# Two products per block of keys in the attention of the second block: both parts of a head's values in one loaded weight

## The chip, the cores and the metric

The kernel runs on one core of one Trainium2 chip. The metric is the device time of one execution in microseconds (us): three executions gave 2305.38, 2310.02 and 2313.08, so the median is 2310.02.

## What is computed

The reference is two transformer blocks one after the other, on 512 tokens of width 1024, in float32. The first block (a gated convolution and a linear recurrence, then a layer of 16384 experts) is not touched. The second block has two attentions side by side, which the code calls A and B, then two gated branches, an output projection and a SwiGLU layer.

```python
def forgetting_attention(q, k, v, log_f):        # A: 8 heads of 64
    c = jnp.cumsum(log_f, axis=1)
    s = einsum('bqhd,bkhd->bhqk', q_i, k) * scale + (c_q - c_k), causal mask
    p = jax.nn.softmax(s, axis=-1)
    return einsum('bhqk,bkhd->bqhd', p, v)

def latent_attention(q_nope, q_rope, k_nope, k_rope, v):   # B: 8 heads, values of 64
    s = (einsum('bqhd,bkhd->bhqk', q_nope, k_nope) + einsum('bqhr,bkr->bhqk', q_rope, k_rope)) * scale
    p = jax.nn.softmax(where(chunk mask, s, NEG_INF), axis=-1)
    return einsum('bhqk,bkhd->bqhd', p, v)
```

## The kernel before

TensorE multiplies in a float32 format that keeps fewer bits than float32. So each operand is split (`split`, lines 93 to 95) into an upper part, which ScalarE rounds and copies, and a lower part, which VectorE forms as the difference. A product of two operands is made of three (`mm3`, lines 111 to 121): upper weight by upper data on line 117, upper weight by lower data on line 119, lower weight by upper data on line 120, all summed in PSUM. Each of them loads its own 128 columns of weights.

`second` (from line 1065) runs the second block. Attention A: for each half of four heads it projects q, k and the values (`va_proj`, split on line 1259), then calls `attend` for each head. The values of a half lie in one tile of 4 x 512 columns (`va`, lines 1236 to 1238): first the upper parts of all four heads, 256 columns for each of the four blocks of 128 keys, then the lower parts. A head is read as the 128 columns of its pair of heads (`d`, line 1287), so that the product gives both heads of the pair on 128 rows, and 64 of these are kept. Attention B: the values of all eight heads are projected in four steps and split whole (512 columns, line 1310) into one tile of upper and one of lower parts (`vb`), and again the pair is read. Each head of B first makes its own q (two blocks of the projection, then the rotation `rope`) and k.

`attend` (lines 1031 to 1063) does one head. For each of four blocks of 128 queries: the logits `S` (three products), the biased logits into a tile `lg` (in A the bias is written into `lg` first, line 1282), the largest, the exponential on ScalarE, the reciprocal on VectorE, the scaling on GpSimd (line 1051), transposes of 128 x 128 into `pt` (line 1054), and the split of `pt` into the tiles `ph` and `pl`. The tile `lg` comes out of a ring of five, `S` and `pt` have two banks of PSUM each, `ph`, `pl` and `o` have one. Then the products with the values go into `o`: for each of the four blocks of keys three products over the 512, 384, 256 and 128 queries that can see that block, 12 products in all. At last ScalarE copies the 64 rows of the head out of `o` (line 1063).

Between the heads stands other work of TensorE: the projections of the gates (`gate_tiles`, two of 24 products for each listed head, `GATE_A` and `GATE_B`), which are started behind the first product of `S` and of `o` of their head (`self.anchor`, an order alone, no wait), the projections of the second half of A, and those of B. The order of the instructions on each engine is planned at build time by the framework's own model of the time line, from the order of the program and from when it thinks operands are ready; the order that is built is then fixed.

Of the kernel before, what the change touches and what calls it, by code (L numbers as in the profile page):

```python
# [7 lines left out]
F32 = mybir.dt.float32  # L8
F32R = mybir.dt.float32r
# [3 lines left out]
AF = mybir.ActivationFunctionType  # L13
ALU = mybir.AluOpType
# [4 lines left out]
P = 128  # L19
T = 512  # L20
# [50 lines left out]
class K:  # L71
# [11 lines left out]
    def v(self, name, i=0, n=1):  # L83
        o, w = VOFF[name]
        return self.vec[:, o + i:o + i + n]
# [944 lines left out]

    def attend(self, q, k, v, nq, scale, bias, out, row, pools):

        nc = self.nc
        wk, pss, pst, psv, unit = pools
        ph, pl = unit("ph").bitcast(F32R), unit("pl").bitcast(F32R)
        for qt in range(nq):
            n = (qt + 1) * P
            s = slice(qt * P, n)
            S = pss.tile([P, T], F32, name="S")
            first = self.mm3(S[:, :n], [(q[0][:, s], q[1][:, s], k[0][:, :n], k[1][:, :n])])  # L1040
            if qt == 0:
                self.anchor = [first]
            lg = wk.tile([P, T], F32, name="lg", bufs=5)
            sm = wk.tile([P, 4], F32, name="sm", bufs=5)
            nc.vector.tensor_tensor_reduce(lg[:, :n], S[:, :n], bias(qt, lg), scale=1.0, scalar=NEG, op0=ALU.add,
                                           op1=ALU.max, accum_out=sm[:, 0:1])
            nc.vector.tensor_scalar(sm[:, 1:2], sm[:, 0:1], -scale, None, op0=ALU.mult)
            nc.scalar.activation(lg[:, :n], lg[:, :n], AF.Exp, bias=sm[:, 1:2], scale=scale,
                                 accum_out=sm[:, 2:3])
            nc.vector.reciprocal(sm[:, 3:4], sm[:, 2:3])  # L1050
            nc.gpsimd.tensor_tensor(lg[:, :n], lg[:, :n], sm[:, 3:4].to_broadcast([P, n]), op=ALU.mult)
            pt = pst.tile([P, 4, P], F32, name="pt", tag="pt")
            for kb in range(qt + 1):
                nc.tensor.transpose(pt[:, kb], lg[:, kb * P:(kb + 1) * P], self.ident)
            self.split(ph[:, :qt + 1, s], pl[:, :qt + 1, s], pt[:, :qt + 1])
        o = psv.tile([P, T], F32, name="o", tag="o")
        for kb in range(nq):
            vh, vl = v(kb)
            s = slice(kb * P, T)
            first = self.mm3(o[:, s], [(vh, vl, ph[:, kb, s], pl[:, kb, s])], start=kb == 0, stop=kb == nq - 1)  # L1060
            if kb == 0:
                self.anchor.append(first)
        nc.scalar.activation(out, o[row:row + 64], AF.Copy)

    def second(self):
        nc, tc, a = self.nc, self.tc, self.a
        hh, hl, x2 = self.hh, self.hl, self.x2
        NQ = T // P
# [4 lines left out]
        with ExitStack() as octx:  # L1073
            op = self.pool("s0", 1, ctx=octx)
            wk = self.pool("swk", 2, ctx=octx)
# [8 lines left out]
            def unit(tag):  # L1084
                return up.tile([P, 4, T], F32, name="u" + tag, tag=tag)
# [33 lines left out]
            for z in range(2):  # L1119
                for tt in range(NQ):  # L1120
                    nc.tensor.matmul(st[:, z, tt:tt + 1], acc[z][:, tt * P:(tt + 1) * P], self.ones[:, :1],
                                     start=True, stop=True)
# [108 lines left out]
            qa, ka, va = [], [], []  # L1231
            for pr in range(4):
                t = unit(f"{pr}").bitcast(F32R)
                qa.append((t[:, 0], t[:, 1]))
                ka.append((t[:, 2], t[:, 3]))
            for half in range(2):
                t = unit(f"v{half}").bitcast(F32R).rearrange("p a (b d) -> p (a b) d", d=256)
                va.append((t[:, :NQ], t[:, NQ:]))

            def qk(dst, scale):  # L1240
                def fn(n, ps):
# [5 lines left out]
            def va_proj(blk):  # L1247
                raw = self.wload(a["w_in2"][6 + blk], 2048)
                w = []
                for z in range(2):  # L1250
                    h, l = self.wsplit(raw[:, z * 1024:(z + 1) * 1024])
                    w += [(h[:, i * 256:(i + 1) * 256], l[:, i * 256:(i + 1) * 256]) for i in range(4)]
                for tt in range(NQ):
                    s = slice(tt * P, (tt + 1) * P)
                    ps = bank(1 + 2 * (tt % 2))
                    self.mm3(ps[:, :256], [(hh[:, k, s], hl[:, k, s], w[k][0], w[k][1]) for k in range(KT)])
                    t = wk.tile([P, 256], F32, name="vt", tag="t3", bufs=3)
                    nc.vector.tensor_scalar(t, ps[:, :256], rt[:, 2, tt:tt + 1], None, op0=ALU.mult)
                    self.split(va[blk][0][:, tt], va[blk][1][:, tt], t)

            for half in range(2):
                if half == 0:
                    for n in range(2):
                        qk(ka, 1.0)(n, zs[4 + n])
                else:
                    self.proj([a["w_in2"][4]], KT, hh, hl, qk(ka[2:], 1.0), lambda n: bank(1 + 2 * n))
                self.proj([a["w_in2"][3 + 2 * half]], KT, hh, hl, qk(qa[2 * half:], 0.125), lambda n: bank(1 + 2 * n))
                va_proj(half)
                for h in range(4 * half, 4 * half + 4):
                    pr, row = h // 2, 64 * (h % 2)  # L1270
                    pq = pr - 2 * half

                    if h == 0:
                        nb = psx.tile([P, T], F32, name="nb", tag="x")
                        nc.tensor.matmul(nb, self.ident[:8, h:h + 1].to_broadcast([8, P]), n8, start=True, stop=True)
                    else:
                        nb = wk.tile([P, T], F32, name="nb")
                        nc.sync.dma_start(nb, n8d[h:h + 1].to_broadcast([P, T]))

                    def bias(qt, b):  # L1280
                        n = (qt + 1) * P
                        nc.vector.scalar_tensor_tensor(b[:, :n], nb[:, :n], cT[:, qt, h:h + 1], mA[:, T - n:],
                                                       op0=ALU.add, op1=ALU.add)
                        return b[:, :n]

                    s = slice(row, row + 64)
                    d = slice(pq * P, (pq + 1) * P)
                    q, k, v = qa[pr], ka[pr], va[half]
                    self.attend((q[0][s], q[1][s]), (k[0][s], k[1][s]),
                                lambda kb: (v[0][:, kb, d], v[1][:, kb, d]), NQ, 1.0, bias,  # L1290
                                yf[s, pr], row, pools)
                    if h in GATE_A:
                        next(gts)

            vb = [unit(f"{i}").bitcast(F32R) for i in range(2)]
# [3 lines left out]
            h, l = uw[:, 0], uw[:, 1]  # L1299
# [6 lines left out]
            for tt in range(NQ):  # L1306
                s = slice(tt * P, (tt + 1) * P)
                ps = psm.tile([P, T], F32, name="mm")
                self.mm3(ps, [(ckn[0][:, s], ckn[1][:, s], h[:, :512], l[:, :512])])
                self.split(vb[0][:, tt], vb[1][:, tt], ps)  # L1310
            for hd in range(8):
                pr, row = hd // 2, 64 * (hd % 2)
                h, l = wqs[hd % 2]
                self.split(h, l, wqu[:, hd * 256:(hd + 1) * 256])
                ps = psm.tile([P, T], F32, name="mm")
                self.mm3(ps, [(h[:, k * P:(k + 1) * P], l[:, k * P:(k + 1) * P], cqn[0][:, k], cqn[1][:, k])
                              for k in range(2)])
                o = rope(rps[hd % 2], ps)
                q = qs[hd % 2]
                self.split(q[0][:96], q[1][:96], o[:96])  # L1320
                h, l = wks[hd % 2]
                self.split(h, l, wkv[:, hd * 64:hd * 64 + P])
                ps = psm.tile([P, T], F32, name="mm")
                self.mm3(ps, [(h[:, :P], l[:, :P], ckn[0], ckn[1])])
                k = ks[hd % 2]
                self.split(k[0][:64], k[1][:64], ps[:64])
                d = slice(pr * P, (pr + 1) * P)
                self.attend((q[0][:96], q[1][:96]), (k[0][:96], k[1][:96]),
                            lambda kb: (vb[0][:, kb, d], vb[1][:, kb, d]), NQ, 96 ** -0.5,
                            lambda qt, _: mB[:, T - (qt + 1) * P:], yb[row:row + 64, pr], row, pools)  # L1330
                if hd in GATE_B:
                    next(gts)
                if hd == GATE_B[-1]:
                    for c in range(4):
                        self.split(hh[:, c], hl[:, c], yf[:, c])
# [8 lines left out]
            for i in range(4):  # L1344
                raw = self.wload(a["w_br"][i], 2048)
                ws = [self.wsplit(raw[:, z * 1024:(z + 1) * 1024]) for z in range(2)]
                for j in range(2):
                    n = 2 * i + j
                    t = []
                    for z in range(2):  # L1350
# [3 lines left out]
                        ps = bank(2 * n + z)  # L1354
# [229 lines left out]
```

## Time and profile before

| | |
|---|---|
| median of three executions | 2310.02 us |
| the profiled execution | 2304.86 us |
| its span | 2302.9 us |
| TensorE busy | 96% of the span |
| VectorE busy | 71% |
| ScalarE busy | 40% |
| GpSimd busy | 22% |
| attention stage with its projections, by the time line | about 1595 to 1860 us |

In the profile PE is TensorE's products, PEld its loads of weights, DVE VectorE, ACT ScalarE, POOL GpSimd. A line such as L119 is a line of the kernel file. The end of a product is modelled, and neighbouring products overlap, so that the distance from one start to the next is what a product costs in a stream. "idle before" is the time in which the engine had nothing running just before that instruction, with the instruction that ended it. The granted clock of TensorE is given as a share of full speed.

### The profile page before, as it was taken

The numbers are of one execution on the slowest core, as the hardware profiler recorded it, in microseconds if no ns is written. First come the engines' busy times: TensorE is split into PE (matmuls) and PEld (weight loads), VectorE is DVE, ScalarE is ACT, GpSimd is POOL, SyncE is SP. The second block draws the span as 40 slices with busy tenths as digits, with TensorE's granted clock in tenths as the row PEclk, the third lists the DMA queues.
The fourth block names the chain that finished last, engine by engine and source line by source line (L and its number), as shares of the span: only waits on it lengthen the run. The fifth ranks groups of instructions, "written<-read, shape, count | busy, mean of one in ns | idle before, by whom it ended". The sixth has DMA issues, their size and how long they took to land.

```text
span 2302.9 us, 29982 instructions
## 1 busy us (share of the span) xinstructions
PE 2217.4 (96%) x11111; PEld 1915.3 (83%) x11111; DVE 1642.9 (71%) x3121; ACT 922.2 (40%) x1345; POOL 507.6 (22%) x444
## 2 busy tenths in 40 slices
PE   6999998999999799999999999999999999999998
PEld 6888798899998777878998998878877878888887
DVE  7785699999788466678698887977666665444423
ACT  3623343354455333333333333454445454333321
POOL 2020023144212322234365552220122100000000
PEclk9989998999999899999999999999999999999999
DMA  7482365588877989889799997842222253222222
GB/s 283 141 289 83 128 213 193 170 301 289 301 270 281 324 291 309 310 295 317 269 383 331 344 331 263 298 162 89 77 71 73 98 183 110 92 97 105 76 88 75
DMA packets 158307, 483.66 MB, mean 210 GB/s; under 512 B 12232, under 2 KB 80456, under 8 KB 128080
## 3 DMA queue, kind: packets, MB, share of 16 engines
q1 hardware_dynamic: 116688, 330.73, 41.0%
q0 software_dynamic: 41472, 151.01, 18.6%
q8 instruction: 87, 1.43, 0.2%
q14 instruction: 60, 0.49, 0.1%
HBM read 429.65 MB, written 52.05 MB: 209 GB/s over the span
## 4 chain that ended last, share of the span: by engine, by line
PE 80%; DVE 8%; issue 6%; POOL 2%; DMA 2%; ACT 1%; SPq 0%; POOLq 0%; DVEq 0%; ACTq 0%
PE mm L117 12%; PE mm L119 12%; PE mm L120 12%; PE act L120 6%; PE act L119 6%; PE act L117 6%; PE po L119 5%; PE po L117 5%; PE po L120 5%; POOL row L645 2%; PE pg L824 2%; PE pg L826 2%; DVE wlo L95 1%; DMA row<-in_eu_dram,gidx 1%; DVE m L560 1%
## 5 line engine op out<-in xcount | busy, mean ns | idle before, releaser
L94 ACT ACTIVATE whi<-raw 128x1024 fp32r<-128x1024 f32 (+1 forms) x415 | 429.3, 1037 | 501.0 <-PE act L119 214.0
L95 DVE TENSOR_TENSOR wlo<-raw,whi 128x1024 fp32r<-128x1024 f32 (+1 forms) x388 | 463.8, 1198 | 221.3 <-ACT whi L94 210.7
L119 PE MATMUL mm<-hl,whi 128*128 128x512 f32 x928 | 367.5, 397 | 4.1 <-DVE hl L990 2.1
L117 PE MATMUL mm<-hh,whi 128*128 128x512 f32 x928 | 366.1, 398 | 4.5 <-ACT hh L475 1.6
L120 PE MATMUL mm<-hh,wlo 128*128 128x512 f32 x928 | 362.5, 396 | 0.0
L120 PE MATMUL act<-hh,wlo 128*128 128x384 f32 x1024 | 346.8, 340 | 8.6 <-DVE wlo L95 7.7
L117 PE MATMUL act<-hh,whi 128*128 128x384 f32 x1024 | 348.1, 340 | 0.0
L119 PE MATMUL act<-hl,whi 128*128 128x384 f32 x1024 | 347.3, 339 | 0.0
L119 PE MATMUL po<-wlo,ch 128*128 128x512 f32 x768 | 305.9, 398 | 3.6 <-DVE wlo L95 3.6
L120 PE MATMUL po<-whi,cl 128*128 128x512 f32 x768 | 300.8, 397 | 0.0
L117 PE MATMUL po<-whi,ch 128*128 128x512 f32 x768 | 282.2, 398 | 18.1 <-ACT ch L94 16.6
L645 POOL DMA_INDIRECT row<-in_eu_dram,gidx x128 | 171.5, 1340 | 479.5 <-DVE row L659 437.0
L645 POOL DMA_INDIRECT row<-in_ev_dram,gidx x128 | 185.3, 1448 | 210.4 <-DVE acc L676 157.3
L119 PEld LDWEIGHTS mm<-hl,whi 128*128 128x128 f32 x928 | 177.0, 191 | 42.7 <-DVE hl L990 3.0
L117 PEld LDWEIGHTS mm<-hh,whi 128*128 128x128 f32 x928 | 176.6, 191 | 42.5 <-ACT hh L475 2.0
L120 PEld LDWEIGHTS mm<-hh,wlo 128*128 128x128 f32 x928 | 176.6, 190 | 36.5 <-DVE wlo L95 0.3
L120 PEld LDWEIGHTS act<-hh,wlo 128*128 128x128 f32 x1024 | 194.7, 190 | 11.2 <-DVE wlo L95 9.3
L94 ACT ACTIVATE ch<-cf 128x384 fp32r<-128x384 f32 x128 | 67.3, 526 | 326.2 <-PE po L119 166.4
L117 PEld LDWEIGHTS act<-hh,whi 128*128 128x128 f32 x1024 | 195.2, 191 | 2.4
L119 PEld LDWEIGHTS act<-hl,whi 128*128 128x128 f32 x1024 | 195.0, 190 | 1.9
L117 PEld LDWEIGHTS po<-whi,ch 128*128 128x128 f32 x768 | 145.3, 189 | 52.5 <-ACT ch L94 17.3
L119 PEld LDWEIGHTS po<-wlo,ch 128*128 128x128 f32 x768 | 145.5, 189 | 38.0 <-DVE wlo L95 4.7
(476 smaller groups left out, 3417.3 us busy)
## 6 DMA issues: line engine op xcount, KB each, us to landing
raw<-in_uT_dram SPq DMA_DIRECT2D x64, 1024.0 KB
raw<-in_v_dram SPq DMA_DIRECT2D x64, 1024.0 KB
raw<-in_w_in_dram SPq DMA_DIRECT2D x26, 1024.0 KB
gdram<-stage SPq DMA_DIRECT2D x24, 1024.0 KB
G<-gdram SPq DMA_DIRECT2D x16, 1536.0 KB
raw<-in_w_gu_dram SPq DMA_DIRECT2D x22, 1024.0 KB
actd<-sp SPq DMA_DIRECT2D x66, 192.0 KB
sp<-actd SPq DMA_DIRECT2D x66, 192.0 KB
```

What stands on the lines that cost most here:

```text
L94: self.nc.scalar.activation(hi, src, AF.Copy)
L95: (eng or self.nc.vector).tensor_tensor(lo, src, hi.bitcast(F32), op=ALU.subtract)
L117: ins = nc.tensor.matmul(out, wh, xh, start=start and i == 0, stop=False)
L119: nc.tensor.matmul(out, wh, xl, start=False, stop=False)
L120: nc.tensor.matmul(out, wl, xh, start=False, stop=stop and i == n - 1)
L560: nc.vector.tensor_tensor(m[:, :n], m[:, :n], m[:, n:2 * n], op=ALU.add)
L645: nc.gpsimd.indirect_dma_start(out=row, out_offset=None, in_=a[n], in_offset=bass.IndirectOffsetOnAxis(ap=gidx[:, k:k + 1], axis=0))
L824: ins = nc.tensor.matmul(ps[:, t], oj[:, q, :, t], oa[:, q, :, t], start=True, stop=False)
L826: nc.tensor.matmul(ps[:, t], oj[:, q, :, t], oi[:, q, :, t], start=False, stop=True)
```

## The change

The upper and the lower part of one head's values (64 columns each) are put side by side in 128 columns, upper first for an even head, lower first for an odd one. One loaded weight then gives, on 128 rows of `o`, the product with the upper part and the product with the lower part. Per block of keys there are two products, one with `ph` and one with `pl`. The half of `o` that belongs to the lower part is copied by ScalarE into a tile `lo`, which is taken out of the ring of `lg`, and VectorE adds it to the other half into the output. `vsplit` writes the parts in that order; the values of B are split in two halves of 256 columns rather than one of 512, into one tile for heads 0 to 3 and one for heads 4 to 7.

```diff
@@ attend
         o = psv.tile([P, T], F32, name="o", tag="o")
         for kb in range(nq):
-            vh, vl = v(kb)
             s = slice(kb * P, T)
-            first = self.mm3(o[:, s], [(vh, vl, ph[:, kb, s], pl[:, kb, s])], start=kb == 0, stop=kb == nq - 1)
-            if kb == 0:
-                self.anchor.append(first)
-        nc.scalar.activation(out, o[row:row + 64], AF.Copy)
+            for p in (ph, pl):
+                first = nc.tensor.matmul(o[:, s], v(kb), p[:, kb, s], start=kb == 0 and p is ph,
+                                         stop=kb == nq - 1 and p is pl)
+                if kb == 0 and p is ph:
+                    self.anchor.append(first)
+        r, lo = slice(row, row + 64), wk.tile([P, T], F32, name="lg", bufs=5)
+        nc.scalar.activation(lo[r], o[64 - row:P - row], AF.Copy)
+        nc.vector.tensor_tensor(out, o[r], lo[r], op=ALU.add)
+
+    def vsplit(self, dst, src):
+
+        d = dst.rearrange("p (q u d) -> p q u d", q=2, u=4)
+        self.split(d[:, :, 0:4:3], d[:, :, 1:3], src.rearrange("p (q u d) -> p q u d", q=2, u=2))
@@ second
-                t = unit(f"v{half}").bitcast(F32R).rearrange("p a (b d) -> p (a b) d", d=256)
-                va.append((t[:, :NQ], t[:, NQ:]))
+                va.append(unit(f"v{half}").bitcast(F32R))
...
-                    self.split(va[blk][0][:, tt], va[blk][1][:, tt], t)
+                    self.vsplit(va[blk][:, tt], t)
...
-                    d = slice(pq * P, (pq + 1) * P)
+                    d = slice((h % 4) * P, (h % 4 + 1) * P)
...
-                                lambda kb: (v[0][:, kb, d], v[1][:, kb, d]), NQ, 1.0, bias,
+                                lambda kb: v[:, kb, d], NQ, 1.0, bias,
...
-                self.split(vb[0][:, tt], vb[1][:, tt], ps)
+                for half in range(2):
+                    self.vsplit(vb[half][:, tt], ps[:, half * 256:(half + 1) * 256])
...
-                d = slice(pr * P, (pr + 1) * P)
+                d = slice((hd % 4) * P, (hd % 4 + 1) * P)
...
-                            lambda kb: (vb[0][:, kb, d], vb[1][:, kb, d]), NQ, 96 ** -0.5,
+                            lambda kb: vb[hd // 4][:, kb, d], NQ, 96 ** -0.5,
```

## Rows read from the trace of the kernel before

**Rows 1.** The page: engines' busy time (first row), and the chain that ended last.

```profile
PE 2217.4 (96%) x11111; PEld 1915.3 (83%) x11111; DVE 1642.9 (71%) x3121; ACT 922.2 (40%) x1345; POOL 507.6 (22%) x444
...
PE 80%; DVE 8%; issue 6%; POOL 2%; DMA 2%; ACT 1%; SPq 0%; POOLq 0%; DVEq 0%; ACTq 0%
```

**Rows 2.** Windows: stretch, length, PE, PEld, DVE, ACT, POOL busy, clock, DMA.

```profile
1595.00:1860.00 265.00, 259.20 (x1312) 210.30 (x1312) 167.53 (x471) 127.65 (x295) 46.48 (x64) 0.99 0.26 87
1604.30:1617.40 13.10, 11.60 (x61) 8.23 (x60) 11.31 (x40) 7.09 (x21) 3.82 (x6) 1.00 0.15 42
1617.35:1620.50 3.15, 3.15 (x7) 2.48 (x8) 2.29 (x10) 1.05 (x4) 0.78 (x1) 0.50 0.39 83
...
1775.15:1783.15 8.00, 8.00 (x47) 6.65 (x46) 6.29 (x23) 5.03 (x15) 1.02 (x2) 1.00 0.26 70
```

**Rows 3.** The critical chain between 1580 and 1860 us, by line.

```profile
by line: PE mm L117 20.7%; PE mm L120 20.1%; PE mm L119 20.1%; PE pt L1054 5.5%; PE S L117 4.1%; PE S L119 3.4%; PE o L117 3.4%; PE o L119 3.3%; PE S L120 3.2%; PE o L120 3.2%; PE ro L1147 2.2%; DVE lg L1282 1.8%; issue 1.1%; DVE lg L1045 0
```

**Rows 4.** The tile o: the third products of A, all sizes, and of B.

```profile
L120 PE MATMUL o<-uph,uv x32: 272/311/402, 1611.2 to 1729.3; 128*128 128x512 f32 x8, 128*128 128x384 f32 x8, 128*128 128x256 f32 x8, 128*128 128x128 f32 x8
...
L120 PE MATMUL o<-uph,u x32: 272/311/397, 1746.3 to 1848.5; 128*128 128x512 f32 x8, 128*128 128x384 f32 x8, 128*128 128x256 f32 x8, 128*128 128x128 f32 x8
```

**Rows 5.** Time line of PE: third products (L120) of one head, and what followed each.

```profile
1699.79 0.39 PE L120 MATMUL o<-uph,uv 128*128 128x512 f32 x1
...
1700.02 0.33 PE L117 MATMUL o<-uph,uv 128*128 128x384 f32 x1
...
1700.37 0.34 PE L120 MATMUL o<-uph,uv 128*128 128x384 f32 x1
...
1700.55 0.29 PE L117 MATMUL o<-uph,uv 128*128 128x256 f32 x1
...
1700.79 0.29 PE L120 MATMUL o<-uph,uv 128*128 128x256 f32 x1
...
1700.91 0.22 PE L117 MATMUL o<-uph,uv 128*128 128x128 f32 x1
...
1701.09 0.28 PE L120 MATMUL o<-uph,uv 128*128 128x128 f32 x1
...
1701.20 0.41 PE L1054 MATMUL pt<-ident,lg 128*128 128x128 f32 x2
```

**Rows 6.** DVE and ACT groups near the added work, and its cover on DVE (last row).

```profile
L95 DVE TENSOR_TENSOR k<-mm,k 64x512 fp32r<-64x512 f32 x7 | 4.8, 680 | 1.0 <-ACT k L94 1.0
...
L95 DVE TENSOR_TENSOR upl<-pt,uph 128x512 fp32r<-128x512 f32 x8 | 5.5, 689 | 1.4 <-ACT uph L94 1.4
...
L95 DVE TENSOR_TENSOR upl<-pt,uph 128x256 fp32r<-128x256 f32 x8 | 3.3, 411 | 0.0
...
L1063 ACT ACTIVATE yf<-o 64x512 f32<-64x512 f32 x8 | 4.7, 589 | 11.7 <-PE o L120 11.7
...
L94 ACT ACTIVATE uph<-pt 128x256 fp32r<-128x256 f32 x16 | 6.0, 373 | 2.2 <-PE pt L1054 2.2
...
1778.20 0.29 DVE L1045 CUSTOM_DVE_ANT_0 lg<-S,mB 128x128 f32<-128x128 f32 x1 [1.08 <-PE S L120]
```

**Rows 7.** Waits between 1595 and 1860 us: total, times, longest.

```profile
DVE lg L1282 <- PE pt L1054: 9.2, 8, 2.7
```

**Rows 8.** Time line of PE: the starts with the longest idle times before them.

```profile
1615.20 0.32 PE L117 MATMUL S<-u 64*128 64x128 f32 x1 [0.78 <-DVE sm L1045]
...
1617.35 0.79 PE L117 MATMUL o<-uph,uv 128*128 128x512 f32 x1 [0.69 <-ACT uph L94]
...
1736.05 0.50 PE L117 MATMUL S<-k,uv 96*128 96x128 f32 x2 [0.93 <-ACT k L94]
...
1854.81 0.50 PE L117 MATMUL mm<-hh,whi 128*128 128x512 f32 x1 [1.35 <-DVE uph L1358]
```

**Rows 9.** Time line of ACT, DVE and PE behind the last head of B.

```profile
1848.84 0.59 ACT L1063 ACTIVATE uv<-o 64x512 f32<-64x512 f32 x1 [5.83 <-PE o L120]
...
1850.13 0.69 DVE L95 TENSOR_TENSOR hl<-uv,hh 128x512 fp32r<-128x512 f32 x1 [5.86 <-ACT hh L94]
...
1850.77 0.60 PE L186 MATMUL xR<-ident,rt 128*128 128x128 f32 x4
```

More of the change, by code (lines that the diff above doesn't have):

```diff
@@ L1270, in second @@
                     pr, row = h // 2, 64 * (h % 2)
-                    pq = pr - 2 * half
                     if h == 0:
```

## The prediction

> **What bounds the kernel now.** I read the page first: TensorE is busy for 96% of the span, and 80% of the chain that ended last is its work [rows 1]. That is an average over very different stages, so the second view is the windows of the stage that the change touches, the two attentions with the projections between them, from 1595 to 1860 us. There TensorE is busy for 259.20 of 265.00 us, VectorE for 167.53, ScalarE for 127.65 [rows 2]. The third view is the chain within that stage: nearly all pieces are products, and the three lines of the tile o have 3.4%, 3.3% and 3.2% of its 280 us [rows 3]. So a product that goes away here shortens the stage, as long as TensorE does not start to wait. The fourth view is where it waits already: the longest idle times before a product are 1.35, 0.93, 0.78 and 0.69 us [rows 8]. Two of these lie in the one stretch where the softmax of the next head sets the pace (1604.3 to 1617.4 us, VectorE busy for 11.31 of 13.10 us and TensorE for 11.60 [rows 2]); one is the start of attention B, one the step behind its last head.
>
> **What is removed.** The third product of every block of keys (line 120): 32 in A and 32 in B, eight of each size in both [rows 4]. What one costs in a stream is the distance from its start to the next start. In one undisturbed head these are 1700.02 - 1699.79 = 0.23 us at 512 columns, 0.18 at 384, 0.12 at 256 and 0.11 at 128 [rows 5], together 0.64 us a head, and 16 x 0.64 = 10.2 us. The chain gives the lower bound: 3.2% of 280 us is 9.0 us on line 120 [rows 3]. Both are near each other; I take 10.2, since TensorE works in order with almost no gap around. The loads of their weights go too, but they run beside other products and are in these distances already. There is a rule that speaks for less. The Trainium skill, "TensorE: Matmul & The Clock Gate", section "Back-to-back issue gap", gives 131 ns for a product of 512 columns and 81 ns for one of 128 in a sustained stream with its loads; by that four products would be worth between 0.32 and 0.52 us a head (an estimate from the two figures), and the sum below would be a gain of about 4 to 7 us. The row has 0.23 us at 512 columns, so the sum goes by the row.
>
> **What is added.** (a) One addition on VectorE for each head, 64 x 512, from PSUM. The nearest row has the same shape, reads PSUM too and takes 680 ns [rows 6], so 16 x 0.68 = 10.9 us of VectorE, which goes from 63% to 67% busy in the stage. The copy by ScalarE stays as long as it was (589 ns [rows 6]): it takes the other half of o. The addition waits for it, and behind it in VectorE's queue stand the largest logit and the lower split of the next head. In a close pair of heads of B VectorE was idle for 1.08 us just there [rows 6], and in the 8.00 us between the first products with the values of these two heads TensorE never waited and VectorE was busy for 6.29 [rows 2]. So this is covered, except where TensorE waits already. At two of these places (1604.3 to 1617.4 us and the start of B) up to 0.68 us can show in full; I take half of it, 0.7 us for both. The bank of o comes free some 0.7 us later, while the next head's first product into it starts 8 us after the previous head's [rows 2].
>
> (b) Behind the last head of B the addition lies on the path: copy at 1848.84, then the split of that output on ScalarE and VectorE, then the branch products [rows 9]. Between 0 (the products that still stand before xR at 1850.77 us cover it) and 0.7 us; the place has an idle time of 1.35 us already [rows 8], so I take 0.5.
>
> (c) The values of B are split in eight pieces of 256, not four of 512. VectorE: 2 x 0.411 - 0.689 = 0.13 us more each, ScalarE: 2 x 0.373 - 0.589 = 0.16 [rows 6], so 4 x 0.29 = 1.2 us if nothing covered it. They lie beside products of gates and of the heads 6 and 7 of A; I take 0, with 1.2 as the other end. The strided order of the pieces has no row; I take the same durations.
>
> (d) The tile lo takes every fifth place of the ring lg. Before, logits could be written as soon as those five tiles back were transposed, which is a tile of one block earlier in the head before; now they wait for the tile of the same block of the head before. The nearest row is the wait of line 1282 for transposes: 9.2 us in 8 waits, 1.15 us each [rows 7]. It ends on VectorE and not on TensorE. Nothing to gain here, since a later transpose cannot release earlier; at most 1.15 us a head, 18.4 us for all. I take 0: outside of the one stretch TensorE has gates and projections to run meanwhile. Uncovered, it comes back as a rival.
>
> No transfer is added or moved, so SP's and GpSimd's queues stay as they are.
>
> **The sum.** -10.2 + 0.7 + 0.5 = -9.0 us. Against the profiled execution (2304.86 us, 2 us over its span) that is 2295.9. The median of the three runs is 5.2 us higher than that execution, so I apply the difference to it: 2310.0 - 9.0 = 2301.0 us, 0.39% less. The three runs lie 7.7 us apart, and about 0.3%, 6.9 us, is what a measurement of this kernel can tell from no change; the forecast is only just beyond it.
>
> **The clock.** After the waits of 0.78 and 0.69 us, from 1617.35 to 1620.50 us, the granted clock is 0.50, which is 1.2 GHz rather than 2.4 [rows 2, 8]. Half of 3.15 us, 1.6 us, was lost there beside the waits. If the new order of that stretch keeps TensorE fed, 0.78 + 0.69 + 1.6 = 3.1 us are gained; each new group of such waits can cost 1.6 on top of itself. The Trainium skill says the same on the page named above, section "HAM oscillation": idle gaps between groups of products bring the half clock back, and it is paid each time. The trace agrees once here, with 0.50.
>
> **The rivals.** First, *some heads become bound by their softmax*. Three heads of sixteen that follow close on one another would not gain their 0.64 and would add 0.68 each, and one more stretch at 1.2 GHz costs 1.6: 3 x 1.32 + 1.6 = 5.6, so -10.2 + 5.6 + 0.5 = -4.1, 2305.9 us, which is no change. For it: 11.31 of 13.10 us of VectorE in one such stretch. Against: 6.29 of 8.00 in another, with no wait of TensorE. Chance 0.30.
>
> Second, on the other side, *the ring bounds*: in A and B the logits of a head wait for the transposes of the head before (d), and this wait reaches TensorE. A head bound in this way does not gain 0.64 and pays 0.68 + 1.15, so 2.47 us. It decides from seven heads on, where 7 x 2.47 = 17.3 less 10.2 is 7.1 us. With nine heads it is +12.0, 2322 us. Against it: the row's waits end on VectorE, which is idle for a third of the stage, and TensorE has other work between most heads. Chance 0.07.
>
> Third, *a product is worth its start and its load, not its columns*: then each removed one is worth the 0.11 us of the smallest [rows 5], 64 x 0.11 = 7.0, and -7.0 + 1.2 = -5.8 gives 2304.2 us. The page's figures point this way; the distances of 0.23 and 0.18 in the rows speak against it. Chance 0.03.
>
> **The numbers.** The forecast, a gain of over 6.9 us, gets 0.60; the first and third rivals end within 0.3%, together 0.33; slower 0.07. The low end is the full 10.2 with the stretch at 1.2 GHz gone as well: 2310.0 - 13.3 = 2296.7, rounded to 2296.5. The high end takes in the first rival and the rest of the unknown costs, (c) in full and part of (d), up to no gain at all with a little scatter: 2311. What is left out is the slower case and a little at either end. The likeliest case alone reaches from 2296.5 to 2303.
>
> **What would show it.** Right: 128 products into o, not 192; line 120 gone from the tile o; the stage from the first logits of A to the first branch product some 9 us shorter; no new idle times of TensorE over 0.5 us in it; the addition on VectorE near 0.68 us, with waits that only ScalarE's copy ends. Wrong: idle times before S or o that VectorE or ScalarE ends, and a granted clock of 0.50 behind them; line 1282 or 1045 waiting longer for transposes; or the same distances between the products, but a longer step behind the last head.

## The result, and the profile after

The changed kernel takes 2335.27 us (median of four, 2332.82 to 2335.59), the kernel before 2309.93. The ratio is 1.0113 with an interval of 1.0097 to 1.0129: slower by about 25 us, where a gain of 9 was forecast. The profiled execution has a span of 2333.4 us, 30.5 more than before.

The page of the changed kernel: its busy times, TensorE's busy share and its granted clock in 40 equal slices (in tenths; 9 is 90% or more), and the chain that ended last:

```profile
PE 2228.8 (96%) x11047; PEld 1916.0 (82%) x11047; DVE 1651.9 (71%) x3141; ACT 924.6 (40%) x1349; POOL 507.3 (22%) x444
...
PE   6999998999999799999999999999999999999998
...
PEclk9989998999999899999999999999999999999999
...
PE 80%; DVE 10%; DMA 6%; issue 2%; ACT 2%; POOL 0%; DVEq 0%; SPq 0%; ACTq 0%; POOLq 0%
```

Beside [rows 1] this page tells almost nothing: TensorE is busy for 96% of the span in both. 64 products are gone (11111 to 11047), and yet its busy time has grown by 11 us. So products have become longer, which points to the clock. The stage shows it. Its windows, after, from the first product of S to the transposes into xR behind the last head (length, then PE, PEld, DVE, ACT, POOL busy, granted clock, DMA); the four below lie within it:

```profile
1596.00:1881.30 285.30, 264.27 (x1223) 205.42 (x1223) 171.10 (x483) 125.11 (x291) 45.81 (x64) 0.94 0.22 76
1614.40:1627.00 12.60, 11.18 (x35) 7.88 (x36) 4.82 (x19) 4.27 (x12) 2.84 (x4) 0.61 0.06 21
1680.00:1690.00 10.00, 8.73 (x29) 5.91 (x29) 6.72 (x24) 5.47 (x16) 2.80 (x4) 0.66 0.08 27
1716.00:1740.00 24.00, 20.38 (x70) 13.61 (x69) 14.84 (x50) 8.80 (x26) 5.01 (x8) 0.79 0.18 66
1825.00:1840.00 15.00, 11.81 (x47) 8.73 (x46) 6.22 (x24) 5.64 (x16) 2.84 (x4) 0.77 0.00 0
```

The same stage of the kernel before:

```profile
1592.50:1850.80 258.30, 253.85 (x1287) 205.37 (x1287) 163.27 (x464) 122.30 (x287) 46.48 (x64) 0.99 0.25 84
```

It is 27.0 us longer, although it holds 64 products less. TensorE is idle for 285.30 - 264.27 = 21.0 us of it (before 4.5), and the granted clock is 0.94 (before 0.99); in four stretches it stands between 0.61 and 0.79, which is a mixture of 1.2 and 2.4 GHz. The other 3.5 us lie ahead of the first S, in code that is the same; that point moves between 1590.6 and 1596.8 us in the runs below, and nothing is concluded from it.

What TensorE waits for, after, between 1590 and 1900 us (total, times, longest):

```profile
PE S L117 <- DVE sm L1046: 4.8, 10, 0.8
PE pt L1055 <- POOL lg L1052: 4.2, 10, 1.2
PE o L1061 <- ACT uph L94: 4.1, 6, 0.7
PE pt L1055 <- DVE upl L95: 3.5, 4, 1.7
```

These are the steps of the softmax, one after the other (`sm` holds the largest logits and the sums, `uph` and `upl` are the upper and the lower part of `pt`): 30 waits, 16.6 us. Before, waits of these four kinds came three times in all, 1.8 us together, the two largest 0.78 and 0.69 us [rows 8]. Idle times before S and o that VectorE or ScalarE ends, with a low clock behind them, are what the prediction had named as the sign of being wrong. Why the softmax is late is seen on VectorE. Before, the first bias of head 1 is written well ahead of the transposes of head 0, and the second as soon as one of them has freed its place:

```profile
1597.03 0.34 DVE L1282 SCALAR_TENSOR_TENSOR lg<-nb,cT,mA 128x128 f32<-128x128 f32 x1
...
1604.31 0.48 DVE L1282 SCALAR_TENSOR_TENSOR lg<-nb,cT,mA 128x256 f32<-128x256 f32 x1 [2.73 <-PE pt L1054]
```

After, at the passage from the first to the second head of A: the two last lower splits of head 0, the four biases of head 1, the first largest logit, and the addition of head 0:

```profile
1611.04 1.24 DVE L95 TENSOR_TENSOR upl<-pt,uph 128x384 fp32r<-128x384 f32 x2 [0.16 <-ACT uph L94]
1612.19 1.93 DVE L1289 SCALAR_TENSOR_TENSOR lg<-nb,cT,mA 128x128 f32<-128x128 f32 x4
1614.04 0.28 DVE L1046 CUSTOM_DVE_ANT_0 lg<-S,lg 128x128 f32<-128x128 f32 x1
...
1614.26 0.68 DVE L1067 TENSOR_TENSOR yf<-o,lg 64x512 f32<-64x512 f32 x1
```

All four biases of head 1 stand together behind the last split of head 0, and the products of head 0 with its values have begun by then (1611.60 us). The softmax of the next head no longer runs beside the end of this one: it starts when that is over, and TensorE stands.

### The profile page after: what moved, and what is told of

Same layout as the page of the kernel before. It is cut to its first block, busy times and chain, and to the rows that moved or that the text cites. A ratio compares the mean times of both kernels' runs of the same rounds, so it can differ in the third digit from the quotient of the medians.

```text
span 2333.4 us, 29859 instructions
## 1 busy us (share of the span) xinstructions
PE 2228.8 (96%) x11047; PEld 1916.0 (82%) x11047; DVE 1651.9 (71%) x3141; ACT 924.6 (40%) x1349; POOL 507.3 (22%) x444
## 3 DMA queue, kind: packets, MB, share of 16 engines
q0 software_dynamic: 41472, 151.01, 18.4%
## 4 chain that ended last, share of the span: by engine, by line
PE 80%; DVE 10%; DMA 6%; issue 2%; ACT 2%; POOL 0%; DVEq 0%; SPq 0%; ACTq 0%; POOLq 0%
PE mm L117 12%; PE mm L119 12%; PE mm L120 12%; PE act L120 6%; PE act L119 6%; PE act L117 6%; PE po L119 6%; PE po L117 6%; PE po L120 6%; DMA sp<-actd 3%; DVE row L659 2%; PE pg L824 2%; PE pg L826 2%; DVE wlo L95 1%; PE pt L1055 1%
## 5 line engine op out<-in xcount | busy, mean ns | idle before, releaser
L120 PE MATMUL mm<-hh,wlo 128*128 128x512 f32 x928 | 364.6, 398 | 0.0
L120 PE MATMUL act<-hh,wlo 128*128 128x384 f32 x1024 | 347.1, 340 | 8.1 <-DVE wlo L95 7.1
L120 PE MATMUL po<-whi,cl 128*128 128x512 f32 x768 | 300.8, 397 | 0.0
L120 PEld LDWEIGHTS mm<-hh,wlo 128*128 128x128 f32 x928 | 178.1, 192 | 37.2 <-DVE wlo L95 0.3
L120 PEld LDWEIGHTS act<-hh,wlo 128*128 128x128 f32 x1024 | 195.0, 191 | 10.3 <-DVE wlo L95 8.4
```

Of the source, the lines that this page charges most:

```text
L120: nc.tensor.matmul(out, wl, xh, start=False, stop=stop and i == n - 1)
```

## The experiments

One sum is made for each run: the length of the stage from the first S to xR, TensorE's idle time in it (length less busy time), and the clock that was not granted (over slices of 3 us, each slice's length times one less its granted clock, added up; idle time at the lower level is in both, so it is rough). What is left is about the time of the products at 2.4 GHz. The places of the gates move some of their products out of the stage or into it, so only rows with the same gates compare closely. All values in us:

| run | stage | idle | clock | left | ratio to before, interval |
|---|---|---|---|---|---|
| before | 258.3 | 4.5 | 1.7 | 252.1 | |
| the change | 285.3 | 21.0 | 17.1 | 247.2 | 1.0113 (1.0097 to 1.0129) |
| addition in place | 256.4 | 6.4 | 6.8 | 243.2 | 0.9992 (0.9982 to 1.0001) |
| before, ring of four | 257.2 | 3.9 | 0.0 | 253.3 | 0.9997 (0.9988 to 1.0006) |
| two products, no addition | 251.3 | 5.4 | 3.4 | 242.5 | 0.9972 (0.9959 to 0.9985) |
| before and a VectorE operation | 256.1 | 3.2 | 1.7 | 251.2 | 0.9997 (0.9983 to 1.0010) |
| before, late tile in the ring | 292.3 | 20.8 | 13.7 | 257.8 | 1.0147 (1.0129 to 1.0166) |
| same places, two rings | 258.3 | 10.1 | 5.1 | 243.1 | 0.9997 (0.9984 to 1.0010) |
| in place, gates 0 4 5 7, 0 3 5 6 | 252.2 | 4.5 | 6.8 | 240.8 | 0.9978 (0.9967 to 0.9989) |
| in place, gates 0 1 5 7, 0 2 4 6 | 256.1 | 9.2 | 5.1 | 241.8 | 0.9990 (0.9979 to 1.0002) |
| in place, gates 0 4 5 7, 0 2 5 6 | 253.5 | 6.3 | 5.1 | 242.1 | 0.9981 (0.9969 to 0.9992) |
| before, gates 0 4 5 7, 0 3 5 6 | 265.8 | 6.0 | 6.8 | 253.0 | 1.0030 (1.0016 to 1.0044) |

**The tile lo out of the ring.**

```diff
-        r, lo = slice(row, row + 64), wk.tile([P, T], F32, name="lg", bufs=5)
-        nc.scalar.activation(lo[r], o[64 - row:P - row], AF.Copy)
-        nc.vector.tensor_tensor(out, o[r], lo[r], op=ALU.add)
+        nc.scalar.activation(out, o[64 - row:P - row], AF.Copy)
+        nc.vector.tensor_tensor(out, o[row:row + 64], out, op=ALU.add)
```

> The change with one thing different: ScalarE copies the lower half of o straight into the output and VectorE adds the upper half to it in place, so no tile is taken out of the ring lg. Ring theory (the fifth place of the ring is what was lost): TensorE's new idle times before S and pt are gone, the granted clock in the stage is back at 0.98 or more, and the forecast holds, a gain of 6 to 10 us on the kernel before (2300 to 2304 us). Rival, the addition on VectorE or the new planned order does the harm: it stays slower than before by 15 us or more. Between the two, both take part.

Measured: 2306.24 us against 2309.11, ratio 0.9992. It lies between the two expectations: the loss of 25 us is gone, but next to nothing of the gain is there. The stage of this run and the same passage on VectorE:

```profile
1592.60:1849.00 256.40, 249.98 (x1222) 200.21 (x1222) 172.89 (x483) 123.92 (x291) 47.22 (x64) 0.97 0.25 85
```

```profile
1597.16 0.35 DVE L1288 SCALAR_TENSOR_TENSOR lg<-nb,cT,mA 128x128 f32<-128x128 f32 x1
...
1604.42 0.49 DVE L1288 SCALAR_TENSOR_TENSOR lg<-nb,cT,mA 128x256 f32<-128x256 f32 x1 [2.71 <-PE pt L1055]
...
1605.40 0.62 DVE L1288 SCALAR_TENSOR_TENSOR lg<-nb,cT,mA 128x384 f32<-128x384 f32 x1 [0.30 <-PE pt L1055]
```

The first bias of head 1 is written at 1597.16 us, long before head 0 is transposed, and the next two follow as places come free. Idle time is back at 6.4 us. So the tile that takes a place in the ring did the harm, and not the products or the addition.

**The ring one place shorter, in the kernel before.**

```diff
-            lg = wk.tile([P, T], F32, name="lg", bufs=5)
+            lg = wk.tile([P, T], F32, name="lg", bufs=4)
```

> The kernel before with four places in the ring lg instead of five, nothing else. Ring theory: the ring alone costs about what the changed kernel lost on the forecast, 25 to 36 us slower than before, with waits before S and pt. Rival (the order or the addition): within 7 us of before.

Measured: 2308.14 us, ratio 0.9997. The ring theory as I had put it falls here. A head of four tiles in a ring of four has exactly the logits' places that the change leaves, and it costs nothing. Its row on VectorE shows the wait that I had priced, and that it harms nobody: the first bias of head 1 comes after 3.23 us of waiting for the first transpose, at 1604.65 us, and still well ahead of the products with the values.

```profile
1604.65 0.35 DVE L1282 SCALAR_TENSOR_TENSOR lg<-nb,cT,mA 128x128 f32<-128x128 f32 x1 [3.23 <-PE pt L1054]
```

**Two products alone.**

```diff
-        r, lo = slice(row, row + 64), wk.tile([P, T], F32, name="lg", bufs=5)
-        nc.scalar.activation(lo[r], o[64 - row:P - row], AF.Copy)
-        nc.vector.tensor_tensor(out, o[r], lo[r], op=ALU.add)
+        nc.scalar.activation(out, o[row:row + 64], AF.Copy)
```

> The change without the addition and without its tile: ScalarE copies the half of o that belongs to the upper parts, and the products with the lower parts of the values are left out of the sum. It shows what two products instead of three bring by themselves. Ring theory and addition theory both: 8 to 11 us faster than before. If the new planned order is to blame: still slower than before.

Measured: 2301.84 us, ratio 0.9972, some 6.5 us faster (2309.11 x 0.0028), a little short of what was expected. In the table the products took 242.5 us against 252.1, so the 9.6 us are there; 2.6 of them went into a little more idle time and clock.

**The addition alone, in the kernel before.**

```diff
         nc.scalar.activation(out, o[row:row + 64], AF.Copy)
+        nc.vector.tensor_tensor(out, o[row:row + 64], out, op=ALU.max)
```

> The kernel before with one more VectorE operation for each head behind ScalarE's copy, of the same shape as the addition (the larger of o and its own copy, in place, which is the same value). Ring theory: 0 to 3 us slower than before. Addition theory: 15 us slower or more.

Measured: 2306.96 us, ratio 0.9997: no cost, as the ring theory said. With the run before this one it leaves a new question: neither the ring's length nor the operation nor the two products cost anything, and the three together cost 25 us. The order on VectorE gave the next theory: the places of a ring are given out in the order of the program. The tile lo of head 0 comes before the logits of head 1 in the program, but is first written when the products with the values are through; so no logits of head 1 get a place until then, however many are free. This happens when the order is planned, not on the chip: in the changed kernel ScalarE writes lo of head 0 at 1613.64 us, the four biases of head 1 had run from 1612.19 us without waiting for it, and only their place in VectorE's order held them.

```profile
1613.64 0.59 ACT L1066 ACTIVATE lg<-o 64x512 f32<-64x512 f32 x1 [2.09 <-PE o L1061]
```

**A late tile in the ring, with nothing else changed.**

```diff
-        nc.scalar.activation(out, o[row:row + 64], AF.Copy)
+        r, lo = slice(row, row + 64), wk.tile([P, T], F32, name="lg", bufs=5)
+        nc.scalar.activation(lo[r], o[r], AF.Copy)
+        nc.vector.tensor_tensor(out, o[r], lo[r], op=ALU.max)
```

> The kernel before, three products as ever, but its output goes through a tile of the ring lg (five places): ScalarE copies the head's half of o into that tile and VectorE takes the larger of the half and its copy, which is the same value. New theory (order of the ring: the places are handed out in the order of the program, so that no logits of the next head get a place before the tile that takes o has its own, and that is first written when the products with the values are through): 25 to 35 us slower than before, and all four biases of the next head in one row behind the last lower split. Rival (the loss came with the two products or with the split of the values): within 5 us of before.

Measured: 2343.13 us against 2308.38, ratio 1.0147, 34 us slower, at the upper end of what was expected. Three products as before, values split as before, and the same picture on VectorE, all four biases in a row behind the last split:

```profile
1613.21 1.23 DVE L95 TENSOR_TENSOR upl<-pt,uph 128x384 fp32r<-128x384 f32 x2 [0.16 <-ACT uph L94]
1614.37 1.93 DVE L1284 SCALAR_TENSOR_TENSOR lg<-nb,cT,mA 128x128 f32<-128x128 f32 x4
...
1617.05 0.68 DVE L1065 TENSOR_TENSOR yf<-o,lg 64x512 f32<-64x512 f32 x1 [0.55 <-ACT lg L1064]
```

**The same places as two rings.**

```diff
-            lg = wk.tile([P, T], F32, name="lg", bufs=5)
+            lg = wk.tile([P, T], F32, name="lg", bufs=4)
...
-        r, lo = slice(row, row + 64), wk.tile([P, T], F32, name="lg", bufs=5)
+        r, lo = slice(row, row + 64), wk.tile([P, T], F32, name="lo", bufs=1)
```

> The change with the same five places of memory, but as two rings: four for the logits, one for the tile lo. Order theory: the loss is gone, 2300 to 2307 us, like the run with the addition in place; the clock at 0.98 or more in the stage. Rival (five places are too few for logits and lo together): as slow as the change, 2330 us or more.

Measured: 2308.52 us, ratio 0.9997; a little over the expected time, with the loss gone. The memory is the same to the byte, and so are the instructions apart from their order; what differs is that lo does not stand in line with the logits. On VectorE the biases of head 1 come one by one again, between the splits of head 0:

```profile
1609.33 0.35 DVE L1289 SCALAR_TENSOR_TENSOR lg<-nb,cT,mA 128x128 f32<-128x128 f32 x1 [3.22 <-PE pt L1055]
1609.70 0.29 DVE L95 TENSOR_TENSOR upl<-pt,uph 128x128 fp32r<-128x128 f32 x1
1610.32 0.48 DVE L1289 SCALAR_TENSOR_TENSOR lg<-nb,cT,mA 128x256 f32<-128x256 f32 x1
```

These two runs settle the cause of the loss: a tile that is written late, in a ring whose other tiles are needed early. The size fits too: the late tile costs 34 us with three products, and with two the change is 27 us slower than the same kernel with two rings (2335.27 and 2308.52 us). That the rule is the order of the program is the reading that fits all the orders; no run shows the planner's own record of it.

**What ate the gain that is left.** In the run with the addition in place the products are 8.9 us shorter in the table, but idle time and clock are 7.0 us more than before. Its longest waits lie at the first heads of A and of B, here on TensorE's time line:

```profile
1615.94 1.26 PE L1055 MATMUL pt<-ident,lg 128*128 128x128 f32 x5 [1.11 <-POOL lg L1052]
...
1734.52 0.49 PE L117 MATMUL S<-k,uv 96*128 96x128 f32 x2 [1.72 <-ACT k L94]
```

So I moved the gates there, which are what TensorE has to do meanwhile.

```diff
-GATE_A = (1, 4, 5, 7)
-GATE_B = (1, 3, 5, 6)
+GATE_A = (0, 4, 5, 7)
+GATE_B = (0, 3, 5, 6)
```

> The run with the addition in place, and the gates of A behind heads 0, 4, 5, 7 and of B behind 0, 3, 5, 6 (before: 1, 4, 5, 7 and 1, 3, 5, 6), so that TensorE has other products at the first heads of both attentions, where that run lost 6.8 us to the granted clock. If those waits are what kept the gain down: 2298 to 2303 us, clock 0.99. If the waits only move to the next heads: 2304 to 2308 us.

Measured: 2303.41 us against 2308.38, ratio 0.9978, faster than both kernels, but at 0.97 and not 0.99 of the clock, and just above the time expected if those waits were all. The wait of 1.72 us at the start of B is gone; other waits stayed, and the clock as well:

```profile
1607.00:1619.00 12.00, 11.21 (x37) 8.13 (x36) 8.45 (x38) 6.53 (x20) 5.59 (x8) 0.58 0.11 24
1775.00:1781.00 6.00, 5.53 (x22) 4.55 (x23) 4.13 (x15) 2.55 (x8) 1.14 (x3) 0.72 0.00 0
```

In the first of these 12.00 x 0.42 = 5.0 us of clock are missing, though TensorE is idle for 0.8 us only.

> The same with the gates of A behind heads 0, 1, 5, 7 and of B behind 0, 2, 4, 6. If an even spread feeds TensorE through both transitions: 2298 to 2303 us. If heads 2 to 4 of A or the last heads then wait: 2305 us or more.

The gates `(0, 1, 5, 7)` and `(0, 2, 4, 6)`: 2304.94 us, ratio 0.9990. Idle time was 9.2 us. Two waits at the first passage of A stayed (0.78 and 0.71 us), and new ones stand between 1690 and 1701 us, at one later passage of A, and at several heads of B: in kind the second of the two expectations, in time at its edge.

> The addition in place, gates of A behind heads 0, 4, 5, 7 and of B behind 0, 2, 5, 6. The run with 0, 3, 5, 6 still waited at head 2 of B and lost 1.7 us to the clock there. If a gate at head 2 covers it: 2 to 3 us faster than that run, near 2301 us. If the wait moves to heads 3 and 4: the same as that run or slower.

The gates `(0, 4, 5, 7)` and `(0, 2, 5, 6)`: 2304.99 us, ratio 0.9981, the same as with `(0, 3, 5, 6)`. The drop of the clock at 1775 us was gone, but idle time grew from 4.5 to 6.3.

> The kernel before with the gates behind heads 0, 4, 5, 7 of A and 0, 3, 5, 6 of B, nothing else: how much of the gain of the run with the addition in place and these gates is the gates' own. If the gates alone do it: 3 to 6 us faster than before. If the two products are needed: within 2 us of before.

The kernel before with these gates (`(0, 4, 5, 7)`, `(0, 3, 5, 6)`): 2315.35 us against 2309.86, ratio 1.0030, about 7 us slower, which neither expectation had. So the gates by themselves bring nothing, and here they cost. With the same gates the two products and their addition are worth 1.0030 - 0.9978 = 0.0052 of 2309, about 12 us.

## Why the prediction was wrong, by its own steps

**What bounds the stage: right.** TensorE bounds it, and what ends its waits is the softmax.

**The removed products, 10.2 us: right.** The time left for the products falls from 252.1 to 243.2, 242.5 and 243.1 us in the three runs without the late tile, so by 8.9 to 9.6, between the two bounds (9.0 and 10.2) or just below. With the moved gates the same difference is 12.2 (253.0 less 240.8), so this measure is good to some 2 or 3 us. The distances after show it directly; the last head of B, two products for each size, 0.23 or 0.22, 0.18 or 0.17, 0.12, 0.06 or 0.11 us apart as in [rows 5]:

```profile
1877.98 0.39 PE L1061 MATMUL o<-uph,u 128*128 128x512 f32 x1
1878.21 0.39 PE L1061 MATMUL o<-upl,u 128*128 128x512 f32 x1
1878.43 0.34 PE L1061 MATMUL o<-uph,u 128*128 128x384 f32 x1
...
1879.08 0.27 PE L1061 MATMUL o<-upl,u 128*128 128x128 f32 x1
1879.19 0.45 PE L117 MATMUL mm<-hh,whi 128*128 128x512 f32 x1
```

The third rival, that a product is worth its start and its load only, does not hold for this stream: 512 columns cost 0.23 us here too, and the removed products were worth more than that rival's 7.0 us. The Trainium skill gives 131 ns for a product of 512 columns in a sustained stream ("TensorE: Matmul & The Clock Gate", section "Back-to-back issue gap"). The trace does not agree: its 0.23 us decide.

**(a) The addition, 0.68 us each and covered: right in size, too small in effect.** It takes 671 to 696 ns. Beside three products it costs nothing (0.9997). Beside two products it seems to cost some 5 us: the stage is 256.4 with it and 251.3 without, and the ratios are 0.9992 and 0.9972, their intervals just meeting. Of these 5.1 us, 1.0 is idle time and 3.4 clock. The planned orders of the two differ as well, so how much is the operation and how much the order stays open.

**(b) The step behind the last head, 0.5 us: no cost was seen.** The last product of o starts at 1879.08 us and xR at 1881.30, 2.2 us later, as it was before (1848.53 and 1850.77). The split of the last head's output does begin 0.8 us later on ScalarE (1.72 us behind the start of that last product, before 0.94), but other products cover it: the longest wait behind it fell from 1.35 to 0.9 us.

**(c) The values of B in eight pieces, 0:** not tried alone. Nothing in the runs without the late tile asks for it.

**(d) The ring, taken at 0: this is the step that failed.** The prediction put it as "now they wait for the tile of the same block of the head before", a shift by one block, priced at 1.15 us a head and covered. That shift is what the ring of four shows, and it is indeed worth nothing. Even its outer bound, 18.4 us, is too low: 25 us slower where 9 were to be gained makes 34. What happens is another thing: lo stands in line between two heads, and the next head's logits are planned behind this head's last split, when its products with the values have begun. It takes away the overlap of one head's softmax with the end of the head before: at all seven passages of A the four biases stand in one row ahead of the addition, and in B the first two largest logits of a head do. Idle time grew by 16.5 us and missing clock by 15.4; 31.9 less the 4.9 by which the rest is shorter is the 27.0 of the stage. That this rest is 4 us longer than in the runs without the late tile goes with the number of waits: the list of TensorE's waits has 41 here and 11 in the run with the addition in place. A product in front of a wait counts with its whole length, where in a stream it counts with the distance to the next one: 0.39 against 0.23 us at 512 columns, 0.27 against 0.11 at 128, in the rows above. Thirty waits more at 0.16 us make 4.8 us, an estimate from these rows that no run tries alone.

**The second rival**, that the ring bounds, had 0.07 and a time of 2322 us. It had the place and the sign right, and TensorE waiting for S behind the ring, but its mechanism was the shift, and its price too low by more than half of the 25 us. The forecast's error is that the ring was read as a number of free places, and never as an order.

**The clock: right in kind, far too small in size.** The prediction priced one more stretch at 1.2 GHz at 1.6 us. Nearly half of the new idle time and clock together is clock: 15.4 of 31.9 us (17.1 us missing against 1.7). The Trainium skill, "TensorE: Matmul & The Clock Gate", section "HAM oscillation", says that idle gaps between groups of products bring the half clock back. The trace agrees, in four long stretches, though none of TensorE's waits there is longer than 1.7 us.

## What to carry to other kernels

With a planner that behaves as this one did, a tile that takes a place in a ring also takes a place in a line: if it is written late and the others are needed early, nothing behind it is planned earlier, however many places are free. Give such a tile a ring of its own, or no tile at all (here the copy went straight into the output), and look in the order of the engines, not at the count of buffers. When a bound engine starts to wait, count its clock as well as its idle time, since here the one cost about as much as the other.

## What was not expected of the hardware

It was not expected how little it takes for the granted clock to fall. In the run with the addition in place and the gates 0 4 5 7 the clock is 0.58 over 12 us with 0.8 us of idle time (the rows above). The time line of TensorE there shows one wait, behind products of S with 128 and 256 columns and transposes; the next product of S with 384 columns is already at the lower level (0.52 us where the same line took 0.33):

```profile
1605.60 0.33 PE L119 MATMUL S<-u 64*128 64x384 f32 x1
...
1607.94 0.27 PE L120 MATMUL S<-u 64*128 64x256 f32 x1
1608.93 0.65 PE L117 MATMUL S<-u 64*128 64x384 f32 x1 [0.72 <-DVE sm L1046]
1609.38 0.52 PE L119 MATMUL S<-u 64*128 64x384 f32 x1
```

In the kernel before with a ring of four it never fell in the stage, with 3.9 us of idle time and a wait of 0.69 us before the products with the values of a head (1617.12 us). So the sum of idle time does not tell it, and the same 0.7 us can cost 0.7 or some 5.7 (with the 5.0 of clock above). What decides was not tried.
